# A hybrid attention and RWKV-7 layer: another order and other ring slots for the planned region

## The chip, the cores and the metric

The kernel runs on one core of one Trainium2 chip. The metric is the device time of one execution in microseconds; the time before is the median of three executions. The engines are named as in the profile: PE multiplies matrices (PEld is its loading of weights), DVE, ACT and POOL work on vectors, SP issues most of the transfers.

## The reference

A decoder layer runs attention and a recurrence beside each other on the same normalized tokens (16 meta tokens ahead of 512 of x, width 1024, 16 heads of 64):

```python
h = layer_norm(concat([meta, x]), ln0_g, ln0_b)                  # 528 x 1024
proj = h @ w_in[l]
q, k, v, zr, gate_att, gate_rwkv = split(proj)
att = swa_one(q, k, v, rel_bias, sinks)      # window 128, T5 bias, one sink a head
rw = rwkv7_time_mix(zr, ...)                 # see below
merged = sigmoid(gate_att) * att + sigmoid(gate_rwkv) * rw
h = layer_norm(ALPHA * h + merged @ w_out[l], ln1_g, ln1_b)
ff = square(relu(h @ w_ff1[l])) @ w_ff2[l]                        # 1024 -> 4096 -> 1024
h = layer_norm(ALPHA * h + ff, ln2_g, ln2_b)
return h[:, N_META:]
# the recurrence, for each head with a state S of 64 x 64:
S = S * w_t + (S @ -kk_t)[..., None] * (kk_t * a_t) + v_t[..., None] * k_t
y_t = S @ r_t
```

All of it is in float32.

## The kernel before

Each float32 product is made of three faster ones. A weight tile `wraw` is fetched by SP (L606, 512 KB), ACT casts it to a rounded high part `whi` (L611), DVE takes the difference `wlo` (L613), and `three` (L453 to L456) multiplies high by high, high by low and low by high with the likewise split tokens `hhi` and `hlo` (made by L815 and L817). The rows of one weight tile are used for two blocks of tokens, of 258, 264, 266 or 512 columns. Smaller products (scores, inverses, the recurrence) are plain fp32 matmuls.

Up to about 570 us the work is recorded first and emitted later. `lead` normalizes x while PE runs `busy` matmuls (L688) on an identity. Then come eight head pairs, each with `rwkv` and `attention`:

- projections (dense and `shifted`), evicted by ACT (L653) and DVE (L656); exponentials, keys and gains on ACT and DVE (L924 to L977); norms by PE (L987 to L989), whose result goes through DVE L992 and L994.
- scores L1031, masked on DVE into G, NT and GR (L1039, L1041, L1045).
- the inverse of each 64-block triangle: 62 steps on POOL (L1122, L1126), transfers through DRAM into `XB`, a transpose of `XB` into `U` on DVE (L1153), `inv3` on PE (L1146), a copy by ACT (L1155), `inv4` on PE (L1151), a copy by ACT (L1157), then the folds L1166 (read by DVE L1171) and L1182 (read by DVE L1186). Beside them the meta tokens' short chain, PE L1194, L1195, L1205, L1209, L1213 with ACT's copies L1200, L1216, L1218 between.
- the recurrence over chunks: a chain of seven `link` matmuls for each pair (L1243). Behind each, DVE scales one head's half of the state (L1225) and ACT the other's (L1228), and the next link reads both.
- attention: scores L1297, bias and mask on DVE (L1302, L1303), the softmax's exponentials on ACT (L1322 to L1340), transposes L1354, outputs L1366.

Then the pairs' results are merged, multiplied by w_out (L1418 to L1420), normalized, and the first part of w_ff1 follows. From there on the MLP and the last norm are written out by hand in code that no table orders (L1601, L1605, L1704, L1798).

`Plan.op` records each operation with what it reads and writes. `Plan.order` (L354) then emits the recorded operations in the order of the table `ORDER` (L91, 3087 numbers of operations), and gives each new buffer the place in its ring that stands next in the table `SLOTS` (L222): eight PSUM banks, two wraw tiles, six halves each of whi and wlo, rows for the evicted projections, and so on. All engines take their instructions in the emitted order, so ORDER sets each engine's queue, and SLOTS which earlier readers a buffer must wait for:

```python
for n in ORDER:
    o = self.ops[n]
    assert all(q in done for q in o.deps)
    for b in o.new:
        i = next(slot)
        was = owner.get((b.ring, i))
        assert was is None or left[was] == 0
        owner[b.ring, i] = b
        b.t = rings[b.ring][i]
```

Neither table has a time in it; they are read as they stand.

Of the kernel before, what the change touches and what calls it, by code (L numbers as in the profile page):

```python
# [76 lines left out]
for _name, _c in ROWS:  # L77
# [14 lines left out]
    0, 1, 26, 2, 3, 127, 5, 128, 4, 67, 30, 29, 27, 131, 68, 6, 34, 69, 7, 36, 8, 28, 42, 243,  # L92
    37, 70, 540, 41, 9, 71, 33, 10, 43, 558, 11, 861, 44, 12, 47, 35, 13, 237, 14, 45, 15, 32, 48, 16,
    46, 17, 31, 49, 18, 19, 20, 364, 60, 21, 72, 22, 50, 23, 61, 38, 24, 51, 73, 25, 62, 52, 63, 53,
    79, 64, 55, 84, 66, 89, 54, 80, 94, 86, 65, 74, 85, 81, 56, 190, 96, 87, 57, 99, 95, 90, 88, 100,
    75, 101, 134, 58, 102, 103, 132, 76, 104, 59, 105, 82, 106, 135, 107, 77, 91, 133, 122, 97, 112, 78, 276, 83,
    92, 117, 171, 98, 109, 113, 136, 108, 114, 118, 137, 110, 93, 115, 111, 124, 138, 116, 123, 119, 139, 40, 120, 142,
    125, 121, 244, 126, 143, 39, 191, 245, 246, 192, 144, 130, 172, 129, 862, 145, 140, 236, 141, 248, 146, 247, 254, 147,
    493, 148, 249, 277, 250, 149, 278, 251, 279, 287, 252, 280, 238, 253, 296, 491, 173, 239, 541, 542, 496, 1182, 255, 812,
    241, 497, 174, 494, 256, 240, 261, 495, 257, 175, 262, 242, 297, 564, 281, 258, 282, 299, 259, 265, 283, 298, 813, 185,  # L100
    266, 264, 288, 300, 284, 180, 263, 267, 597, 289, 184, 272, 285, 260, 290, 268, 176, 301, 567, 270, 1133, 271, 183, 273,
    307, 291, 492, 182, 275, 565, 302, 1200, 269, 178, 186, 274, 308, 286, 292, 188, 313, 568, 566, 309, 293, 193, 314, 303,
    337, 315, 294, 316, 559, 322, 560, 879, 561, 317, 336, 338, 179, 329, 562, 323, 326, 569, 333, 328, 194, 330, 570, 342,
    582, 327, 339, 571, 181, 177, 341, 334, 563, 575, 340, 332, 1454, 295, 572, 583, 304, 576, 324, 584, 310, 573, 325, 365,
    586, 577, 574, 331, 600, 578, 196, 195, 343, 311, 335, 345, 579, 601, 498, 585, 580, 366, 367, 197, 598, 198, 588, 346,
    521, 305, 587, 499, 581, 863, 599, 1503, 589, 206, 543, 347, 312, 500, 348, 591, 368, 592, 369, 370, 371, 199, 372, 373,
    501, 374, 375, 522, 376, 377, 318, 200, 523, 378, 596, 201, 379, 380, 526, 381, 382, 544, 383, 207, 384, 344, 545, 385,
    208, 306, 524, 386, 319, 209, 203, 387, 525, 527, 388, 212, 214, 546, 389, 502, 390, 547, 602, 391, 603, 150, 392, 393,
    528, 394, 395, 396, 608, 397, 609, 398, 399, 217, 604, 400, 202, 401, 529, 205, 402, 204, 403, 187, 404, 349, 405, 153,
    354, 406, 215, 548, 154, 407, 216, 408, 549, 218, 409, 814, 410, 610, 411, 151, 412, 550, 210, 413, 152, 357, 414, 213,  # L110
    617, 415, 353, 551, 416, 352, 417, 211, 418, 355, 419, 611, 350, 420, 530, 421, 161, 358, 422, 423, 162, 424, 425, 605,
    426, 427, 163, 428, 606, 429, 815, 155, 430, 607, 351, 593, 219, 620, 594, 612, 164, 189, 613, 320, 590, 165, 220, 432,
    595, 614, 431, 156, 356, 621, 221, 615, 618, 157, 552, 816, 222, 616, 433, 166, 508, 223, 435, 619, 639, 321, 503, 864,
    509, 643, 506, 640, 634, 504, 505, 434, 507, 649, 685, 450, 513, 635, 158, 511, 636, 510, 637, 224, 512, 817, 1455, 225,
    159, 818, 452, 638, 226, 646, 657, 359, 647, 659, 436, 885, 227, 658, 648, 453, 228, 437, 645, 454, 650, 438, 644, 455,
    651, 439, 456, 160, 865, 660, 819, 654, 661, 440, 514, 662, 167, 663, 820, 515, 655, 516, 821, 866, 653, 451, 656, 517,
    822, 652, 686, 168, 628, 169, 360, 457, 170, 441, 362, 518, 363, 867, 458, 629, 688, 886, 687, 2096, 888, 229, 887, 361,
    630, 889, 459, 519, 869, 443, 918, 442, 230, 868, 531, 520, 870, 689, 842, 533, 690, 823, 691, 692, 231, 444, 233, 693,
    232, 694, 234, 532, 695, 696, 447, 445, 697, 698, 446, 829, 919, 699, 449, 700, 824, 701, 920, 702, 534, 448, 703, 825,
    704, 827, 460, 705, 826, 631, 706, 828, 462, 707, 832, 622, 708, 833, 830, 709, 623, 461, 710, 535, 711, 921, 463, 712,  # L120
    624, 834, 464, 465, 831, 713, 625, 835, 714, 466, 715, 626, 871, 468, 716, 467, 922, 536, 717, 836, 845, 469, 938, 718,
    872, 1134, 837, 470, 719, 720, 721, 890, 722, 471, 896, 723, 632, 724, 838, 472, 725, 891, 473, 726, 846, 897, 727, 843,
    633, 892, 728, 474, 537, 729, 664, 844, 730, 475, 666, 627, 1206, 731, 477, 476, 893, 732, 733, 478, 538, 734, 479, 480,
    735, 839, 894, 736, 481, 840, 895, 737, 482, 539, 738, 880, 739, 939, 740, 665, 741, 923, 742, 883, 743, 898, 881, 744,
    745, 483, 746, 680, 747, 841, 484, 748, 882, 749, 899, 750, 485, 486, 751, 903, 924, 1209, 904, 925, 667, 929, 900, 884,
    901, 906, 930, 487, 753, 670, 684, 908, 752, 907, 931, 668, 910, 1775, 1207, 926, 1210, 905, 932, 909, 683, 675, 1208, 933,
    754, 847, 672, 912, 914, 941, 756, 934, 682, 1135, 917, 488, 911, 848, 902, 913, 915, 489, 940, 553, 676, 490, 927, 755,
    955, 554, 916, 928, 678, 942, 852, 873, 943, 671, 555, 1239, 853, 956, 771, 935, 674, 849, 556, 679, 773, 936, 557, 673,
    850, 669, 681, 957, 757, 958, 677, 1006, 1521, 979, 937, 774, 851, 959, 758, 964, 775, 854, 759, 978, 980, 776, 965, 760,
    777, 969, 971, 761, 772, 1136, 778, 972, 762, 1240, 968, 981, 780, 975, 982, 944, 1183, 977, 984, 763, 983, 945, 764, 949,  # L130
    779, 976, 946, 967, 966, 768, 970, 1007, 765, 770, 1184, 855, 766, 2466, 2814, 1137, 950, 767, 1140, 769, 1138, 1008, 1009, 947,
    1139, 781, 1241, 1141, 1185, 783, 782, 784, 856, 785, 786, 951, 858, 1010, 787, 973, 1011, 952, 1012, 789, 948, 1013, 1242, 1244,
    788, 1014, 1015, 1243, 790, 1016, 641, 792, 791, 1245, 1163, 235, 1017, 1018, 793, 1019, 1142, 1020, 794, 795, 642, 1021, 857, 1022,
    1186, 796, 1023, 1143, 953, 1024, 797, 974, 798, 1025, 1187, 1026, 799, 1144, 859, 1027, 800, 801, 1028, 1029, 802, 860, 1030, 803,
    1031, 954, 1145, 1032, 1033, 1150, 1034, 1148, 1035, 1201, 1153, 804, 1036, 1146, 1037, 1188, 1246, 1147, 1038, 1204, 1149, 1039, 1151, 987,
    1202, 1203, 1040, 805, 1211, 1041, 1224, 1154, 1155, 1152, 1217, 1776, 1042, 1156, 1212, 1043, 1044, 1213, 806, 1045, 1157, 807, 985, 1225,
    1158, 1218, 1219, 1189, 1046, 1227, 1190, 808, 1259, 1047, 989, 1166, 1048, 2417, 1049, 960, 874, 1167, 1050, 1191, 1504, 1051, 1159, 1052,
    1053, 1214, 1054, 1164, 1055, 1220, 1056, 988, 1165, 1057, 1250, 986, 875, 1527, 1221, 1058, 1247, 1842, 1262, 1160, 1059, 1060, 1222, 996,
    1161, 1061, 1263, 1168, 1062, 1215, 1063, 999, 1064, 1216, 991, 1065, 1248, 1251, 1233, 1066, 1226, 1249, 1067, 997, 1068, 1169, 1069, 1260,
    1070, 1071, 1261, 1205, 1072, 1252, 1530, 1231, 1456, 809, 1505, 1232, 1253, 1192, 961, 1254, 1162, 1229, 1073, 1074, 1255, 1170, 990, 1531,  # L140
    994, 1824, 1228, 1235, 1193, 1230, 1457, 1234, 1223, 1458, 1171, 1075, 1459, 1238, 1256, 1077, 1237, 1460, 1276, 992, 1257, 1172, 1506, 1528,
    1461, 1277, 1258, 993, 998, 1278, 1236, 1279, 1194, 1270, 1076, 1529, 810, 1285, 995, 1280, 1292, 1299, 1288, 1301, 1286, 1484, 811, 1290,
    1462, 1293, 1300, 1289, 876, 1092, 1302, 1509, 1463, 1296, 1094, 1510, 1000, 1304, 1303, 877, 1173, 1305, 1291, 1271, 1174, 1175, 962, 1078,
    1464, 1281, 1287, 1264, 1298, 1485, 963, 1328, 1079, 1465, 1327, 1297, 1095, 1176, 1080, 1282, 1486, 1096, 1081, 1093, 1295, 1097, 1272, 1082,
    1330, 1329, 1098, 1273, 1265, 1274, 1001, 1275, 1507, 1294, 1099, 1002, 1508, 1083, 1101, 1100, 1005, 1848, 1522, 1331, 1004, 1084, 1332, 1003,
# [1887 lines left out]
```

## Time and profile before

| | us |
|---|---|
| median of three runs | 897.17 (896.90 to 897.31) |
| profiled execution, time | 897.01 |
| profiled execution, span | 895.2 |
| PE busy | 874.7 |
| DVE busy | 674.4 |
| ACT busy | 518.8 |
| POOL busy | 263.2 |

The span runs from the first to the last instruction of the profile, and 1.8 us of the time lie outside it. The mean granted clock of PE was 0.994 of full speed. Busy time of PE is from modelled ends of its matmuls, which overlap, so that short waits between two of them need not show as idle; the time from the start of one to the start of the next does show them. A row of the timeline gives start, length, engine, line, what is written and read, and in brackets the idle time ahead of it with what ended it.

### The profile page before, as it was taken

How to read it: one execution, taken by the hardware profiler on the slowest of the kernel's cores; microseconds unless marked ns; L12 is line 12 of the kernel's file. 1: busy time of each engine (PE TensorE's matmuls, PEld its weight loads, DVE VectorE, ACT ScalarE, POOL GpSimd, SP SyncE). 2: the span in 40 equal slices, each digit the busy share in tenths (PEclk: the TensorE clock that was granted, in tenths of full speed). 3: DMA queues.
4: the chain of work that ended last, by engine and by line, in shares of the span. 5: the costliest groups of instructions: out<-in, count | busy, mean ns of one | idle time of the engine just before them, and what ended most of it. 6: DMA issues, size and time to landing. Idle time of an engine off the chain costs nothing.

```text
span 895.2 us, 17524 instructions
## 1 busy us (share of the span) xinstructions
PE 874.7 (98%) x6712; PEld 768.1 (86%) x6712; DVE 674.4 (75%) x1192; ACT 518.8 (58%) x1131; POOL 263.2 (29%) x672
## 2 busy tenths in 40 slices
PE   7999999999999999999989999999999999999996
PEld 6999989888898998887878877988898989888885
DVE  6882976868868678478497689598877896788757
ACT  7854568466575494483663745765556655564710
POOL 3138164183461721822816502000010000000001
PEclk9999999999999999999989999999999999999999
DMA  7443323424143242223243631395687578576322
GB/s 272 127 130 104 86 75 107 117 64 131 55 123 101 78 109 85 84 70 101 72 109 102 197 102 59 97 299 132 178 209 216 141 202 256 133 209 165 98 91 94
DMA packets 73533, 115.87 MB, mean 129 GB/s; under 512 B 40311, under 2 KB 47737, under 8 KB 69481
## 3 DMA queue, kind: packets, MB, share of 16 engines
q1 hardware_dynamic: 69728, 98.89, 35.5%
q0 software_dynamic: 2880, 14.68, 9.0%
q8 instruction: 53, 0.87, 0.4%
q10 hardware_dynamic: 840, 1.17, 0.4%
q14 instruction: 32, 0.25, 0.1%
HBM read 107.56 MB, written 8.21 MB: 129 GB/s over the span
## 4 chain that ended last, share of the span: by engine, by line
PE 90%; DVE 8%; issue 1%; ACT 1%; DMA 1%; POOL 0%; DVEq 0%; SPq 0%; ACTq 0%
PE g L454 12%; PE g L455 11%; PE g L456 11%; PE dnR L1798 7%; PE rq L1704 5%; PE tp L1704 4%; PE dnP L1798 4%; PE last L1798 4%; PE dnT L1798 3%; PE up L454 3%; PE up L455 3%; PE up L456 3%; PE g L1243 2%; PE g L1182 2%; PE g L1297 2%; PE g L1031 1%
## 5 line engine op out<-in xcount | busy, mean ns | idle before, releaser
L454 PE MATMUL g<-hhi,whi 128*128 128x512 f32 (+3 forms) x640 | 213.1, 333 | 0.2 <-DVE GR L1045 0.2
L455 PE MATMUL g<-hlo,whi 128*128 128x512 f32 (+3 forms) x640 | 204.0, 319 | 1.6 <-DVE hlo L817 1.6
L456 PE MATMUL g<-hhi,wlo 128*128 128x512 f32 (+3 forms) x640 | 203.6, 318 | 0.0
L454 PEld LDWEIGHTS g<-hhi,whi 128*128 128x128 f32 x640 | 121.0, 189 | 12.6 <-issue 2.2
L455 PEld LDWEIGHTS g<-hlo,whi 128*128 128x128 f32 x640 | 121.2, 189 | 9.6 <-DVE hlo L817 2.1
L456 PEld LDWEIGHTS g<-hhi,wlo 128*128 128x128 f32 x640 | 120.9, 189 | 8.5 <-DVE wlo L613 0.2
L613 DVE TENSOR_TENSOR wlo<-wraw,whi 128x512 fp32r<-128x512 f32 x126 | 88.3, 708 | 30.4 <-ACT whi L611 29.9
L1122 POOL TENSOR_TENSOR ftmp<-Xf,Nf 108x84 f32<-108x84 f32 (+23 forms) x248 | 86.8, 350 | 74.9 <-DMA Nf<-Nd 45.9
L611 ACT CAST whi<-wraw 128x512 fp32r<-128x512 f32 x126 | 77.0, 619 | 54.0 <-PE g L455 24.6
L1126 POOL TENSOR_TENSOR Xf<-Xf,ftmp 108x84 f32<-108x84 f32 (+23 forms) x248 | 89.6, 361 | 19.0
L1788 POOL DMA_DIRECT2D braw<-in_w_ff_dram x12 | 10.7, 890 | 206.1 <-DVE wlo L1605 87.2
L1228 ACT ACTIVATE Z<-g,PC 64x64 f32<-64x64 f32 x64 | 19.7, 308 | 65.2 <-DVE Z L1225 39.9
L1267 POOL TENSOR_TENSOR rs<-rs,mhalf 128x8 f32<-128x8 f32 (+1 forms) x9 | 14.9, 1659 | 76.2 <-DVE rs L1266 76.2
L1605 DVE TENSOR_TENSOR wlo<-wraw,whi 128x1024 fp32r<-128x1024 f32 x22 | 26.9, 1222 | 13.2 <-ACT whi L1601 10.6
L1225 DVE TENSOR_SCALAR Z<-g,PC 64x64 f32<-64x64 f32 x64 | 17.6, 274 | 23.3 <-PE g L1243 20.8
L1601 ACT CAST whi<-wraw 128x1024 fp32r<-128x1024 f32 x22 | 22.9, 1042 | 17.5 <-PE dnR L1798 8.7
L1605 DVE TENSOR_TENSOR wlo<-braw,whi 128x1024 fp32r<-128x1024 f32 x25 | 30.5, 1219 | 2.4 <-ACT whi L1601 2.4
L1605 DVE TENSOR_TENSOR blo<-braw,bhi 128x1024 fp32r<-128x1024 f32 x25 | 30.5, 1219 | 1.6 <-ACT bhi L1601 1.5
L1601 ACT CAST whi<-braw 128x1024 fp32r<-128x1024 f32 x25 | 26.3, 1053 | 5.4 <-PE rq L1704 4.6
L656 DVE SCALAR_TENSOR_TENSOR res<-g,vc,res 128x256 f32<-128x256 f32 (+2 forms) x34 | 16.2, 481 | 17.0 <-ACT res L653 16.8
L1601 ACT CAST bhi<-braw 128x1024 fp32r<-128x1024 f32 x25 | 26.3, 1051 | 3.4 <-DMA braw<-in_w_ff_dram 3.4
L454 PE MATMUL up<-h1hi,whi 128*128 128x512 f32 x72 | 28.1, 390 | 0.0
(532 smaller groups left out, 2469.6 us busy)
## 6 DMA issues: line engine op xcount, KB each, us to landing
wraw<-in_w_in_dram SPq DMA_DIRECT2D x52, 512.0 KB
braw<-in_w_ff_dram SPq DMA_DIRECT2D x19, 1024.0 KB
wraw<-in_w_ff_dram SPq DMA_DIRECT2D x32, 512.0 KB
braw<-in_w_ff_dram POOLq DMA_DIRECT2D x12, 1024.0 KB, 8.8
wraw<-in_w_out_dram SPq DMA_DIRECT2D x14, 256.0 KB
Nf<-Nd SPq DMA_DIRECT2D x24, 144.0 KB
res<-in_x_dram SPq DMA_DIRECT2D x4, 512.0 KB
G<-in_consts_dram SPq DMA_DIRECT2D x16, 128.0 KB
```

Of the source, the lines that this page charges most:

```text
L454: pe.matmul(ps, whi, xhi, start=first, stop=False)
L455: pe.matmul(ps, whi, xlo, start=False, stop=False)
L456: pe.matmul(ps, wlo, xhi, start=False, stop=last)
L611: AC(512, lambda hi=hi, qs=qs: act.copy(hi.t, raw.t[:, qs]), plain=True, r=[raw], w=[hi], new=[hi])
L613: f = lambda hi=hi, lo=lo, qs=qs, e=e: e.tensor_tensor(lo.t, raw.t[:, qs], hi.t.bitcast(F32), op=ALU.subtract)
L1122: sub(nj * nt, lambda s=s, nj=nj, nt=nt, tv=tv: pool.tensor_tensor(tv(), Xf.t[:, 0:nj, s : s + 1].to_broadcast([NB, nj, nt]), Nf.t[:, s : ...
L1126: sub(nj * nt, lambda s=s, nj=nj, tv=tv: pool.tensor_tensor(Xf.t[:, 0:nj, s + 1 :], Xf.t[:, 0:nj, s + 1 :], tv(), op=ALU.add), port=1, r=[ ...
L1228: op("ACT", 335, lambda: act.activation(Z.t[H2[1], c, 1, :], src(1), AF.Copy, scale=PC.t[H2[1], last : last + 1]), r=[ps, PC], w=[(Z, ("s" ...
L1601: act.copy(like(s["r"][0][:, :n], s["x"]), s["x"])
L1605: dve.tensor_tensor(lo, s["x"], hi.bitcast(F32), op=ALU.subtract)
L1704: pe.matmul(o, l[:, ks], r[:, k], start=start and k == c == 0, stop=stop and k == 3 and c == 2, skip_group_check=True)
L1798: pe.matmul(acc[b], l[:, as_], r[:, ws], start=first and i == 0 and q == 0, stop=last and i == NP - 1 and q == 2, skip_group_check=True)
```

## The change

Both tables are replaced by others of the same length; no other line differs, and every line number stays:

```diff
 ORDER = [
-    0, 1, 26, 2, 3, 127, 5, 128, 4, 67, 30, 29, 27, 131, 68, 6, 34, 69, 7, 36, 8, 28, 42, 243,
...
+    131, 132, 0, 27, 6, 26, 2, 134, 67, 133, 68, 135, 1, 41, 69, 7, 8, 9, 10, 11, 3, 12, 13, 14,
...
```

So the same operations run, in another sequence on each engine and with other buffers. Where that shows is best seen in the engines' rows at three places. A row gives the line, the operation, what is written and read, the shape, and how often it stands in succession.

PE in the recurrence of pair 5, before. `Z` is the state, `G` the chunk's matrix; the L1096 rows are transposes, and L454 to L456 a projection:

```order
L1031 MATMUL g<-G_143,BK_140 128x128 x8
L1243 MATMUL g<-Z_180,G_144 128x128
L1096 MATMUL g<-con,res_127 128x128 x4
L1243 MATMUL g<-Z_180,G_144 128x128 x3
L454 MATMUL g<-hhi,whi 128x512
L455 MATMUL g<-hlo,whi 128x512
L456 MATMUL g<-hhi,wlo 128x512
```

and in the new order, where L1366 are outputs of attention:

```order
L1031 MATMUL g<-G_143,BK_140 128x128 x16
L1243 MATMUL g<-Z_179,G_144 128x128
L1366 MATMUL g<-pall_194,vtok_216 64x128 x2
L1366 MATMUL g<-pown_195,vdif_218 64x128 x2
L1366 MATMUL g<-pall_194,vtok_216 64x128 x2
L1366 MATMUL g<-pown_195,vdif_218 64x128 x2
L1243 MATMUL g<-Z_179,G_144 128x128 x2
L454 MATMUL g<-hhi,whi 128x512
L455 MATMUL g<-hlo,whi 128x512
L456 MATMUL g<-hhi,wlo 128x512
```

Two links in succession are left there instead of three, and where two stood at the end of this chain there is a projection between now.

PE in pair 6's inverse, before (`U` is what L1153 transposed, `XB` the inverse's blocks):

```order
L1205 MATMUL g<-SVm_166,AKm_168 16x64 x2
L1297 MATMUL g<-khi_214,e_133 128x256 x4
L1209 MATMUL g<-RHm_174,XTm_176 16x64 x2
L1146 MATMUL g<-U_185,NT_162 32x32 x16
L1213 MATMUL g<-SVm_166,BTm_172 64x64 x2
L1151 MATMUL g<-XB_181,U_185 32x32 x16
L454 MATMUL g<-hhi,whi 128x266
L455 MATMUL g<-hlo,whi 128x266
L456 MATMUL g<-hhi,wlo 128x266
```

and in the new order:

```order
L1205 MATMUL g<-SVm_166,AKm_168 16x64 x2
L1146 MATMUL g<-U_185,NT_162 32x32 x16
L454 MATMUL g<-hhi,whi 128x266
L455 MATMUL g<-hlo,whi 128x266
L456 MATMUL g<-hhi,wlo 128x266
L454 MATMUL g<-hhi,whi 128x266
L455 MATMUL g<-hlo,whi 128x266
L456 MATMUL g<-hhi,wlo 128x266
L1209 MATMUL g<-RHm_174,XTm_177 16x64 x2
L1151 MATMUL g<-XB_181,U_185 32x32 x16
```

Between L1146 and L1151, with ACT's copy between them, there now stand six matmuls of 266 columns and the meta chain's L1209.

DVE at the same place, before:

```order
L1045 TENSOR_TENSOR GR_165<-g,con 64x4x64
L1370 SCALAR_TENSOR_TENSOR e_134<-e_134,g 128x512
L1039 TENSOR_TENSOR NT_163<-g,dv_154 64x256
L977 SCALAR_TENSOR_TENSOR res_127<-res_126,vc,e_132 128x512
L1039 TENSOR_TENSOR NT_163<-g,dv_154 64x256
L1153 STREAM_TRANSPOSE U_185<-XB_181 32x256 x2
L1198 TENSOR_TENSOR BTm_172<-g,dvm_155 48x128
L1039 TENSOR_TENSOR NT_163<-g,dv_154 64x256
```

and in the new order, where L1302 is attention's mask:

```order
L1039 TENSOR_TENSOR NT_163<-g,dv_151 64x256
L1045 TENSOR_TENSOR GR_165<-g,con 64x4x64
L1041 TENSOR_TENSOR G_144<-g,con 64x8x64
L613 TENSOR_TENSOR wlo<-wraw,whi 128x512
L1045 TENSOR_TENSOR GR_165<-g,con 64x4x64
L1153 STREAM_TRANSPOSE U_185<-XB_181 32x256 x2
L1045 TENSOR_TENSOR GR_165<-g,con 64x4x64
L1041 TENSOR_TENSOR G_144<-g,con 64x8x64
L1198 TENSOR_TENSOR BTm_172<-g,dvm_155 48x128
```

The transpose L1153 has moved from among pair 7's masks of the scores L1039 (`NT`) to behind all four of them.

ACT ahead of pair 5's inverse, before (L1340 scales the softmax's rows, L1200 and L1216 copy for the meta chain):

```order
L1101 COPY Z_180<-g 64x4x64
L963 COPY BK_140<-BK_140 64x8x64
L1101 COPY Z_180<-g 64x4x64 x2
L1200 COPY SVm_167<-g 16x128
L1089 COPY GR_165<-g 64x4x64
L653 ACTIVATE res_127<-g,drv 128x264
L1013 CAST rk_136<-e_133 128x512
L1216 COPY RHm_175<-g 16x128
L1155 COPY U_185<-g 32x256 x2
```

and in the new order:

```order
L1276 ACTIVATE z_206<-g,vc 128x512
L1089 COPY GR_164<-g 64x4x64
L611 CAST whi<-wraw 128x512
L1358 COPY pall_194<-g 128x512
L611 CAST whi<-wraw 128x512
L1340 ACTIVATE sb_193<-sb_193,sm_197 128x128 x4
L1200 COPY SVm_167<-g 16x128
L653 ACTIVATE e_131<-g,drv 128x264
L1155 COPY U_185<-g 32x256 x2
```

Ahead of L1155 there are now two casts of weights and an eviction for pair 6 (L653), and the second half of the softmax's scaling L1340 stands close to it, where short copies and one eviction stood.

At the very start, SP's first transfer is now the tile of weights of the first projection (L606, wraw), ahead of meta (L693) and the four blocks of x (L682); before, it was the eighth, behind them. Its casts on ACT and its differences on DVE are now the first work of both on data.

318 rows, old and new, of tables (ORDER, SLOTS) are left out of this document.

## The prediction

> **What bounds the kernel now.** I read the busy table first, then the chain that ended last, then the windows, and last the waits of PE. The busy table and the chain's shares by engine:
>
> ```profile
> PE 874.7 (98%) x6712; PEld 768.1 (86%) x6712; DVE 674.4 (75%) x1192; ACT 518.8 (58%) x1131; POOL 263.2 (29%) x672
> PE 90%; DVE 8%; issue 1%; ACT 1%; DMA 1%; POOL 0%; DVEq 0%; SPq 0%; ACTq 0%
> ```
>
> PE is the bound, and since the same instructions run afterwards, all that a new order can win is PE's waiting, the time its clock was low, and what a change between kinds of matmul costs. The windows (span, PE busy with its count, granted clock, DMA share, GB/s) say where PE is idle:
>
> ```profile
> 0.00:100.00 100.00, 93.73 (x711) 1.00 0.49 146
> 400.00:500.00 100.00, 94.73 (x853) 0.97 0.37 103
> 570.00:850.00 280.00, 280.00 (x1583) 1.00 0.65 183
> ```
>
> From 570 us on run the rest of the MLP and the last norm, whose code the tables don't touch (the first half of it is in the last row): 325 us that stay. In 0 to 100 PE is idle 6.3 us, in 400 to 500 it is 5.3. That is not all, for the modelled ends of matmuls hide short waits. The waits for ACT inside the pairs, seen from PE's weight loads (total, times, longest), show some of these:
>
> ```profile
> PEld g L1243 <- ACT Z L1228: 4.7, 10, 1.0
> ...
> PEld g L1151 <- ACT U L1155: 0.8, 2, 0.6
> ...
> PEld g L1213 <- ACT XB L1157: 0.5, 2, 0.4
> ...
> PEld g L1166 <- ACT XB L1157: 0.4, 1, 0.4
> ```
>
> **The change part by part.** First the links of the recurrence. PE's timeline for pair 5 has three of them with nothing in between:
>
> ```profile
> 409.19 0.47 PE L1243 MATMUL g<-Z,G 128*128 128x128 f32 x2
> 410.37 0.49 PE L1243 MATMUL g<-Z,G 128*128 128x128 f32 x2 [0.71 <-ACT Z L1228]
> 411.57 0.49 PE L1243 MATMUL g<-Z,G 128*128 128x128 f32 x2 [0.71 <-ACT Z L1228]
> ```
>
> From one start to the next 1.18 and 1.20 us pass: the link, DVE's half of the scaling (L1225), ACT's half (L1228), the next link. PE needs some 0.95 us of other work behind each link, and where the planner put less, the rest is lost: 4.7 us by the row above. In the new order I went through all 56 links: where pairs 4 and 7 had two triples of 264 columns as cover, some 0.7 us, there is now 1.17 us or more, and in pair 5 one bare pair of links is left where three stood. That pair costs 0.9 us (by the 0.71 above, and up to 1.0 by the row's longest). Gain 3.8 us, with the cover in both cases the projections' matmuls, which run anyway. Should ACT reach L1228 late, the cover is too short again, at the same price a link.
>
> Second, pair 6's inverse, where PE stands behind DVE:
>
> ```profile
> 454.98 1.02 PE L987 MATMUL g<-con,res 128*128 128x2 f32 x8 [0.38 <-DVE res L656]
> 457.65 0.60 PE L1031 MATMUL g<-G,BK 64*128 64x128 f32 x6 [0.31 <-DVE d L992]
> 462.15 0.39 PE L1209 MATMUL g<-RHm,XTm 16*16 16x64 f32 x4
> 463.72 0.24 PE L1146 MATMUL g<-U,NT 32*32 32x32 f32 x2 [1.18 <-DVE U L1153]
> 464.19 1.06 PE L1146 MATMUL g<-U,NT 32*32 32x32 f32 x30 [0.22 <-DVE U L1153]
> 466.08 1.06 PE L1151 MATMUL g<-XB,U 32*32 32x32 f32 x32 [0.42 <-ACT U L1155]
> 462.78 0.43 DVE L1039 TENSOR_TENSOR NT<-g,dv 64x256 f32<-64x256 f32 x1
> 463.24 0.90 DVE L1153 STREAM_TRANSPOSE U<-XB 32x256 f32<-32x256 f32 x2
> ```
>
> The transpose L1153 started right behind L1039, with no idle time: it stood in DVE's queue and not at a transfer. The windows (PE, PE's loads, DVE, ACT, POOL, clock, DMA share, GB/s) show that DVE was full all along, and that the clock then fell:
>
> ```profile
> 455.00:460.00 5.00, 4.69 (x57) 4.19 (x59) 4.97 (x11) 2.59 (x7) 1.41 (x6) 1.00 0.53 141
> 460.00:465.00 5.00, 3.60 (x57) 2.76 (x56) 4.81 (x13) 0.51 (x2) 0.57 (x4) 0.92 0.46 120
> 465.00:470.00 5.00, 4.43 (x55) 3.91 (x52) 4.47 (x10) 4.13 (x9) 0.00 (x0) 0.50 0.63 193
> ```
>
> The new order runs the end of pair 6's preparation earlier and stands two triples of 266 columns between L1146 and L1151 and two more behind L1151, where there was one short or none. Of DVE's work, 24.7 us belonged to 20 us of PE work here (each instruction counted with its own duration); it is spread over 30 us now. So I count the five waits above, 1.8 us of the inverse and 0.7 of L987 and L1031 before it, as gone: 2.5 us. What is late next there is DVE again, at pair 6's scores.
>
> Third, the clock. In the low stretch, and for comparison near 272 us, two neighbours of the same shape each:
>
> ```profile
> 468.53 0.43 PE L455 MATMUL g<-hlo,whi 128*128 128x266 f32 x1
> 468.76 0.42 PE L456 MATMUL g<-hhi,wlo 128*128 128x266 f32 x1
> 272.83 0.29 PE L456 MATMUL g<-hhi,wlo 128*128 128x266 f32 x1
> 272.95 0.28 PE L454 MATMUL g<-hhi,whi 128*128 128x266 f32 x1
> 400.31 0.69 PE L1151 MATMUL g<-XB,U 32*32 32x32 f32 x32
> ```
>
> The start-to-start time is 0.23 against 0.12 us. Twelve such lie in the stretch (1.3 us), and 62 small ones of the inverse took 2.12 us where at full clock they would take 1.34 (0.8); with L1213 and part of L1166 about 2.5 us, an estimate between 2.1 (these two alone) and 3.4 (half of the 6.8 us of low clock). I take the drop as gone with the waits that went ahead of it. The Trainium skill, "TensorE: Matmul & The Clock Gate" (sections "Part 1: The HAM clock gate" and "Why this matters for your kernels"), lays a drop to one whole idle window of about 3.4 us and asks for no idle gaps above about 3 us; the trace disagrees, since here no wait was over 1.18 us and PE was busy 3.60 of 5 us. By the page no stall that I foresee could lower the clock, and the term for new stalls would be a little smaller; by the row a run of narrow matmuls with a wait of one microsecond can.
>
> Fourth, the inverses of the other pairs. The rows for L1151, L1213 and L1166 sum to 1.7 us, of which 0.6 was pair 6's. The new order has 1.0 us of cover or more in each, but in pair 5 L1209 and L1213 now stand next to each other and wait for ACT's copy between them, some 0.3 us. Gain 0.8.
>
> Fifth, changes of the kind of matmul. A 512-column fp32r matmul behind an fp32 one costs
>
> ```profile
> 271.11 0.48 PE L454 MATMUL g<-hhi,whi 128*128 128x512 f32 x1
> 271.43 0.40 PE L455 MATMUL g<-hlo,whi 128*128 128x512 f32 x1
> 271.66 0.39 PE L456 MATMUL g<-hhi,wlo 128*128 128x512 f32 x1
> ```
>
> 0.32 us instead of 0.23. Counted along PE's rows, there are 38 changes between fp32r and fp32 fewer and 4 changes of tiling fewer. Were each worth 0.09, that is 3.8 us at most; but the fp32 matmul that follows another kind starts sooner by about as much, so I take 0.5 (ends 0 and 3.8).
>
> Sixth, the lead. The first wraw block, 512 KB, now goes ahead of meta and x on SP, and ACT's two casts and DVE's two differences for it stand ahead of the layer norm. Before, DVE started at once when x came, and PE later waited for hlo (timeline, the first window, and the group of DVE's differences):
>
> ```profile
> 5.93 1.29 DVE L728 BATCH_NORM_STATS2 stx<-res 128x6 f32<-128x512 f32 x2 [5.93 <-DMA res<-in_x_dram]
> 20.68 0.39 PE L455 MATMUL g<-hlo,whi 128*128 128x264 f32 x1 [1.43 <-DVE hlo L817]
> 0.00:10.00 10.00, 5.50 (x24) 5.21 (x25) 3.39 (x9) 6.99 (x16) 4.13 (x19) 1.00 0.82 275
> L613 DVE TENSOR_TENSOR wlo<-wraw,whi 128x512 fp32r<-128x512 f32 x126 | 88.3, 708 | 30.4 <-ACT whi L611 29.9
> ```
>
> 512 KB at 275 GB/s are 1.9 us by which x can come later; against it, 1.4 us of DVE and 1.2 us of ACT work leave the crowded 10 to 20 us, and the 1.43 us wait may shrink. I take 0, ends -1.4 and +1.9.
>
> Seventh, waits that the new order makes. Nothing in the trace shows them; I looked for them by adding each engine's durations along PE's rows. ACT is the worst: ahead of pair 5's inverse (L1155, L1157) it gets two softmaxes, exponentials and five casts close together. Its groups (busy, mean ns) and its window before:
>
> ```profile
> L611 ACT CAST whi<-wraw 128x512 fp32r<-128x512 f32 x126 | 77.0, 619 | 54.0 <-PE g L455 24.6 <-DMA wraw<-in_w_in_dram 15.5 <-PE g L1420 5.8
> L1326 ACT ACTIVATE sb<-sb,sm 128x128 f32<-128x128 f32 x64 | 24.9, 391 | 0.3
> L1326 ACT ACTIVATION_READ_ACCUMULATOR sb<-sb,sm 128x1 f32 x64 | 12.1, 189 | 0.0
> L1340 ACT ACTIVATE sb<-sb,sm 128x128 f32<-128x128 f32 x64 | 20.4, 394 | 3.1 <-DVE sm L1334 3.1
> 380.00:400.00 20.00, 20.00 (x187) 18.32 (x187) 15.55 (x34) 17.33 (x47) 5.11 (x22) 1.00 0.26 69
> ```
>
> Eight of L1326 with their reads (4.6 us), eight of L1340 (3.2), five of L611 (3.1) and some 14 us of copies and activations make 24.8 us for 20 us of PE work; before, ACT was busy 17.33 of these 20. It could arrive up to 4.8 us late, less what of it can start early (in the 10 us ahead it has only 1.7 us to do). From 430 to 450 it is 22.7 us for 20, ahead of pair 6's scores. Ends 0 and 4.8 + 2.7 = 7.5; I take 3.5, half, since ACT's queue is nearly empty ahead of the first and PE's order has 1.0 us of cover behind L1146.
>
> The sum: -3.8 - 2.5 - 2.5 - 0.8 - 0.5 + 0 + 3.5 = -6.6 us. The profiled execution took 897.01 us (span 895.2), the median of the runs is 897.17, so both give 890.5.
>
> **The rivals.** (a) Slower: ACT is as late as it can be at both places, 4.8 and 2.7 us, and each time PE waits in the midst of 64- and 32-row matmuls, so that the clock falls for a while as at 464 us (2.5 us each): +12.5 instead of +3.5, or 899.4. It decides as soon as ACT's lateness and its clock drops eat more than the 10.1 us won. For it speaks that ACT's work cannot be hurried and that pair 5's inverse, scores and folds are a long stretch of narrow matmuls; against it that much of that ACT work has its inputs long before. (b) No change: the gains come, but DVE becomes what PE waits for in its new crowded places. Along PE's rows I count 12.2 us of DVE work in 90 to 100, 11.4 in 280 to 290, 12.5 in 330 to 340 and 11.5 in 440 to 450, each of 10; were each excess a wait, +7.6 beside +3.5 for ACT less 1 us of overlap, and the time 897. Against it speaks that most of them follow a slack stretch (3.4 us at 80 to 90, 6.0 at 320). (c) More: no new waits, the clock whole, and the lead and the mode changes at their good ends: -9.6 - 1.4 - 2.0 = -13, or 884.
>
> **How the numbers follow.** The forecast's case, a gain with part of it given back, 887 to 894, holds 0.52; (c) and what lies below 887 hold 0.17; a small gain of 894 to 895.4 holds 0.05. Within 0.2% (1.8 us, about what a measurement of this kernel can tell from no change) lie (b) and weak forms of (a) with 0.11, and above 899 lies (a) with 0.15. So faster 0.74, same 0.11, slower 0.15. The range leaves out the worst of (a) and the best of (c): 883.5 to 898.
>
> **What would show it.** Links: PE's loads wait for ACT Z L1228 about once and under 1.2 us in total. Pair 6: no wait of L1146 for L1153 over 0.3 us and granted clock 1.00 from 400 to 500. ACT: waits of L1151, L1166, L1182 or L1031 for ACT between 395 and 455 of up to 3.5 us in all. Lead: x's first statistics start near 7.5 us, and the first projection no later than 2 us after where it was. I am wrong if the clock falls elsewhere, or if PE's idle time up to 570 us does not fall by about half.

## The result and the profile after

The new order takes 909.85 us (median of 4 runs, 908.63 to 913.52) against 897.04 for the old: a ratio of 1.0149, 95% interval 1.012 to 1.0179. It is slower by 12.8 us, where 6.6 less were forecast. The profiled execution took 909.41 us (span 906.5). Its runs also lie further apart than those of the old order, which stay within 0.5 us here (within 2.5 to 5 us in the later rounds). All medians are of runs in the faster state; one run of e13 (924.53 us, granted clock 0.977) was in a slower one and isn't counted.

The busy table after:

```profile
PE 875.9 (97%) x6712; PEld 768.8 (85%) x6712; DVE 676.6 (75%) x1192; ACT 518.2 (57%) x1131; POOL 292.7 (32%) x672
```

PE, DVE and ACT do the same as before to within 2.2 us of busy time. POOL is busy 292.7 us where it was 263.2, with the same 672 instructions. Two groups hold nearly all of that; first of the old order, then of the new:

```profile
L1126 POOL TENSOR_TENSOR Xf<-Xf,ftmp 108x84 f32<-108x84 f32 (+23 forms) x248 | 89.6, 361 | 19.0
L1122 POOL TENSOR_TENSOR ftmp<-Xf,Nf 108x84 f32<-108x84 f32 (+23 forms) x248 | 86.8, 350 | 74.9 <-DMA Nf<-Nd 45.9 <-DMA wraw<-in_w_in_dram 11.5
```

```profile
L1126 POOL TENSOR_TENSOR Xf<-Xf,ftmp 108x84 f32<-108x84 f32 (+23 forms) x248 | 108.5, 437 | 18.4
L1122 POOL TENSOR_TENSOR ftmp<-Xf,Nf 108x84 f32<-108x84 f32 (+23 forms) x248 | 97.5, 393 | 137.2 <-DMA Nf<-Nd 97.1 <-DMA G<-in_consts_dram 13.1 <-DMA bias<-tbd 9.1
```

These are the 62 steps of each pair's inverse: 176.4 us in all before, 206.0 after, on the same operands. Where PE waits (line, releaser, total, times, longest), first two rows of the old order, then the new:

```profile
PE g L1243 <- ACT Z L1228: 2.2, 3, 0.8
...
PE g L1146 <- DVE U L1153: 1.4, 2, 1.2
```

```profile
PE g L688 <- DMA con<-in_consts_dram: 5.1, 1, 5.1
PE g L1273 <- issue: 4.4, 1, 4.4
PE g L1146 <- DVE U L1153: 4.0, 4, 2.0
PE g L1194 <- ACT e L1376: 1.7, 1, 1.7
PE g L776 <- ACT sb L770: 1.4, 1, 1.4
PE g L1151 <- ACT U L1155: 1.0, 1, 1.0
PE g L1205 <- ACT SVm L1200: 1.0, 1, 1.0
...
PE g L1243 <- ACT Z L1228: 0.7, 1, 0.7
```

The links wait 0.7 us where they waited 2.2, and pair 6's L1146, whose two waits made up the 1.4 us, no longer waits. But L1146 waits in pairs 0 and 5, and DVE's transpose ahead of it no longer stands in DVE's queue. It waits for its transfer, which it never did before (here the new order's row of what DVE was idle for before L1153):

```profile
  DMA XB<-xtd: 7.1, 7
```

From the end of a pair's loop to the start of its first transpose the old order has 12.8 to 18.1 us; the new order has 6.1 to 16.4, least in pairs 0 and 5 (6.1 and 6.5), the two where PE then waits at L1146.

And in place of one stretch of low clock ahead of the MLP (464 to 471 us) there are three (107.3 to 114.1, 407.7 to 417.9 and 506.7 to 513.5 us), each with waits at or near its start. The windows (span, PE busy, granted clock, DMA share, GB/s):

```profile
105.00:115.00 10.00, 7.93 (x102) 0.66 0.39 128
400.00:420.00 20.00, 16.77 (x210) 0.74 0.33 88
500.00:515.00 15.00, 10.62 (x40) 0.77 0.43 130
```

Why POOL's steps take longer is seen by laying POOL's rows beside DVE's at one place, pair 5's loop:

```profile
383.18 0.38 POOL L1126 TENSOR_TENSOR Xf<-Xf,ftmp 108x91 f32<-108x91 f32 x1
383.63 0.74 POOL L1122 TENSOR_TENSOR ftmp<-Xf,Nf 108x84 f32<-108x84 f32 x1
384.45 0.70 POOL L1126 TENSOR_TENSOR Xf<-Xf,ftmp 108x84 f32<-108x84 f32 x1
385.23 0.66 POOL L1122 TENSOR_TENSOR ftmp<-Xf,Nf 108x77 f32<-108x77 f32 x1
385.97 1.99 POOL L1126 TENSOR_TENSOR Xf<-Xf,ftmp 108x77 f32<-108x77 f32 x1
388.03 0.33 POOL L1122 TENSOR_TENSOR ftmp<-Xf,Nf 108x80 f32<-108x80 f32 x1
```

```profile
383.50 2.20 DVE L613 TENSOR_TENSOR wlo<-wraw,whi 128x512 fp32r<-128x512 f32 x3
385.62 0.29 DVE L956 SCALAR_TENSOR_TENSOR AXm<-res,drv,Pm 64x16 f32<-64x16 f32 x1
385.84 0.67 DVE L613 TENSOR_TENSOR wlo<-wraw,whi 128x512 fp32r<-128x512 f32 x1
386.44 0.69 DVE L946 SCALAR_TENSOR_TENSOR e<-res,res 128x528 f32<-128x528 f32 x1
387.06 0.69 DVE L947 TENSOR_TENSOR res<-res,res 128x528 f32<-128x528 f32 x1
```

A step that takes 0.35 us alone takes 0.7 us beside each L613, and 1.99 us beside L613, L946 and L947 in succession. All of these have two operands in SBUF. A fit over all 992 steps of both traces (each step's duration beyond the shortest of its line and shape, against the time that each DVE line ran beside it) gives 0.7 us of stretch for each us of L613, and at most 0.1 for L656, L1186, L1302 and L1041, which read PSUM. Summed, the stretch is 26 us in the old order and 56 in the new: the new one has 40 us of L613 beside loops where the old order has 30, and more of L946, L947, L952 and their like.

The Trainium skill, "SBUF — State Buffer" (section "SBUF: two separate sides"), states that DVE with two SBUF inputs and a POOL instruction that reads SBUF exclude each other for the length of the instruction; these rows agree (0.35 us becomes 1.99).

### The profile page after: what moved, and what is told of

The parts are those of the page before. It is cut to its first block, busy times and chain, and to the rows that moved or that the text cites. A ratio compares the mean times of both kernels' runs of the same rounds, so it can differ in the third digit from the quotient of the medians.

```text
span 906.5 us, 17479 instructions
## 1 busy us (share of the span) xinstructions
PE 875.9 (97%) x6712; PEld 768.8 (85%) x6712; DVE 676.6 (75%) x1192; ACT 518.2 (57%) x1131; POOL 292.7 (32%) x672
## 5 line engine op out<-in xcount | busy, mean ns | idle before, releaser
L454 PE MATMUL g<-hhi,whi 128*128 128x512 f32 (+3 forms) x640 | 211.1, 330 | 0.0
L456 PE MATMUL g<-hhi,wlo 128*128 128x512 f32 (+3 forms) x640 | 203.4, 318 | 0.5 <-DVE wlo L613 0.5
L1122 POOL TENSOR_TENSOR ftmp<-Xf,Nf 108x84 f32<-108x84 f32 (+23 forms) x248 | 97.5, 393 | 137.2 <-DMA Nf<-Nd 97.1
L454 PEld LDWEIGHTS g<-hhi,whi 128*128 128x128 f32 x640 | 120.9, 189 | 9.3 <-issue 0.9
L456 PEld LDWEIGHTS g<-hhi,wlo 128*128 128x128 f32 x640 | 120.7, 189 | 9.3 <-DVE wlo L613 0.9
L1126 POOL TENSOR_TENSOR Xf<-Xf,ftmp 108x84 f32<-108x84 f32 (+23 forms) x248 | 108.5, 437 | 18.4
L613 DVE TENSOR_TENSOR wlo<-wraw,whi 128x512 fp32r<-128x512 f32 x126 | 89.9, 723 | 30.2 <-ACT whi L611 20.0
L611 ACT CAST whi<-wraw 128x512 fp32r<-128x512 f32 x126 | 76.2, 618 | 58.1 <-DMA wraw<-in_w_in_dram 30.6
L1228 ACT ACTIVATE Z<-g,PC 64x64 f32<-64x64 f32 x64 | 19.8, 309 | 67.9 <-PE g L1243 40.5
L1225 DVE TENSOR_SCALAR Z<-g,PC 64x64 f32<-64x64 f32 x64 | 17.5, 274 | 36.4 <-ACT Z L1228 22.6
L1267 POOL TENSOR_TENSOR rs<-rs,mhalf 128x8 f32<-128x8 f32 (+1 forms) x9 | 14.4, 1602 | 46.8 <-DVE rs L1266 46.8
L1418 PE MATMUL g<-whi,hhi 128*128 128x512 f32 x64 | 27.9, 436 | 0.5 <-DVE e L1380 0.5
L653 ACT ACTIVATE res<-g,drv 128x264 f32<-128x264 f32 (+1 forms) x32 | 14.9, 476 | 23.0 <-PE g L456 22.6
```

The lines of the kernel that those rows point to most:

```text
L454: pe.matmul(ps, whi, xhi, start=first, stop=False)
L456: pe.matmul(ps, wlo, xhi, start=False, stop=last)
L611: AC(512, lambda hi=hi, qs=qs: act.copy(hi.t, raw.t[:, qs]), plain=True, r=[raw], w=[hi], new=[hi])
L613: f = lambda hi=hi, lo=lo, qs=qs, e=e: e.tensor_tensor(lo.t, raw.t[:, qs], hi.t.bitcast(F32), op=ALU.subtract)
L1122: sub(nj * nt, lambda s=s, nj=nj, nt=nt, tv=tv: pool.tensor_tensor(tv(), Xf.t[:, 0:nj, s : s + 1].to_broadcast([NB, nj, nt]), Nf.t[:, s : ...
L1126: sub(nj * nt, lambda s=s, nj=nj, tv=tv: pool.tensor_tensor(Xf.t[:, 0:nj, s + 1 :], Xf.t[:, 0:nj, s + 1 :], tv(), op=ALU.add), port=1, r=[ ...
```

## The experiments

Each changes the old or the new order in one respect; what a kernel leaves out is said in its expectation. Times are medians, with the ratio to the old order's runs beside them and its interval.

**Is it POOL's loops?** In e1 and e2 the 60 steps behind a loop's first two are left out:

```diff
-            sub(nj * nt, lambda s=s, ...: pool.tensor_tensor(
+            sub(nj * nt, lambda s=s, ...: None if s else pool.tensor_tensor(
```

In e3 and e4 the first ten multiplications are done twice, with the same result:

```diff
-            sub(nj * nt, lambda s=s, ...: pool.tensor_tensor(tv(), ..., op=ALU.mult), ...
+            sub(nj * nt, lambda s=s, ...: [pool.tensor_tensor(tv(), ..., op=ALU.mult) for _ in range(2 if s < 10 else 1)], ...
```

> The new order with 60 of the 62 POOL steps of each pair's inverse left out (its output is therefore not the layer's). Theory POOL: the new order loses because POOL ends its inverse loops late (its steps stretch beside DVE's L613), so that DVE's transpose L1153, PE's L1146 and L1194 and POOL's own L1267 come late; without the steps the waits at 105, 232, 404 and 504 us (about 11.5 us) and the clock drops behind three of them go: 892, range 888 to 896. Rival ORDER (ACT's and DVE's queues are what PE waits for, POOL only looks late): 904 to 910. Rival LEAD (the first transfers): 908.

> The old order with the same 60 steps left out in each pair. Theory POOL: the old order has 13 to 18 us between a loop's end and the transpose, so its loops aren't on the path: 894 to 897. Rival ORDER: the same. If POOL's steps cost both orders alike (contention with DVE at large), it falls as much as the new order does, to about 885.

> The old order with ten POOL multiplications of each pair's loop done twice (the same result), some 4 us more in each loop. Theory POOL: absorbed by the slack of 13 to 18 us, of which the transfers need about 7: 897 to 899. Rival (no slack matters, POOL's load itself costs): +4 or more.

> The new order with the same 4 us more in each loop. Theory POOL: pairs 0, 2 and 5 and the step L1267 behind pair 7's loop have no slack, so each pays about 4 us, the others less: 920 to 930. Rival ORDER: 910 to 914.

Measured: e1 886.44 us (0.9879, 0.9862 to 0.9897), e2 896.62 (0.9992, 0.9982 to 1.0002), e3 917.16 (1.0218, 1.0187 to 1.0249), e4 919.91 (1.0251, 1.0232 to 1.0271). Without the loops the new order is 10.2 us faster than the old, and its waits of PE shrink. The three largest that are left:

```profile
PE g L688 <- DMA con<-in_consts_dram: 5.5, 1, 5.5
PE g L455 <- DVE hlo L817: 0.9, 3, 0.4
PE g L1243 <- ACT Z L1228: 0.7, 1, 0.7
```

The clock stays whole up to the MLP. So the loss hangs on POOL's loops: 23.4 us of the new order's time, and nothing clear of noise of the old one's. But e3 was a miss: I had taken the 13 to 18 us between the end of a loop and the transpose for slack, and some 3.4 us more in a loop cost the old order 20 us. That POOL's load itself costs this much is e3's rival; e2 speaks against it, for there nearly all of that load goes and nothing is gained. What the trace of e3 shows is lateness: L1267 and other POOL work stand behind steps, and weight transfers stand on SP behind L1130, which waits for the loop's end (SP waited for L1126 48 us there, 40 before). PE then waited 3.0 us at L1273 and 4.2 for whi and wlo. How the 20 us divide among these was not measured. The old order too is cut to the length that its loops have.

**Length, or something else?** e5, e9 and e10 replace all but a loop's first two steps by fills that read nothing:

```diff
-            sub(nj * nt, lambda s=s, ...: pool.tensor_tensor(tv(), ...), ...
+            sub(nj * nt, lambda s=s, ...: pool.tensor_tensor(tv(), ...) if s == 0 else [pool.memset(tmp.t, 0.0) for _ in range(nt_)], ...
-            sub(nj * nt, lambda s=s, ...: pool.tensor_tensor(Xf..., tv(), op=ALU.add), ...
+            sub(nj * nt, lambda s=s, ...: pool.tensor_tensor(Xf..., tv(), op=ALU.add) if s == 0 else [pool.memset(Xf.t, 0.0) for _ in range(nx_)], ...
# fills of tmp and of Xf in each step: e5 2 (1 from step 20 on) and 1; e9 1 and 2; e10 2 and 2
```

> The new order with all but the first two POOL steps of each loop replaced by fills that read nothing (the inverse's values are left out), made so that a loop lasts about 28 us by the trace's fill times, as the old order's loops do. Theory STRETCH (the loops are late because POOL's reading steps stand still beside DVE instructions with two operands in SBUF): the fills don't stretch, 888 to 894. Rival PLACE (the loops' place in the new order is too late at any usual length): 902 to 910.

> The new order with fills in place of POOL's steps again (the inverse's values are left out), now longer: about 27.6 us a loop by the fills' times, as the old order's loops are (27 to 29 without their gaps), with nothing to read in SBUF. Theory STRETCH (the new order is right for loops of the old length, and loses by the 3 to 5 us that each loop is stretched): 887 to 893. Rival (a loop of this length is already too late in the new order): 900 to 907.

> The same with 31.3 us a loop, the length that the steps have in the new order (30.6 to 32.6 us in most pairs). Theory STRETCH: the length alone brings the loss back, 904 to 912. Rival (not the loops' length but the standing still itself, or POOL holding up DVE): as the run with 27.6 us, within 3 us.

Measured: e5 886.27 us (0.9875, 0.9862 to 0.9888), but its loops came out shorter than meant, 19 to 22 us in five of the eight pairs; e9 889.35 (0.9914, 0.9893 to 0.9934) with loops of 28 to 31 in six; e10 931.4 (1.0376, 1.0344 to 1.0409) with 35 to 40 in seven, longer than meant. The fills' own length hardly depends on what DVE does (min, median, max in ns, e9):

```profile
L1129 POOL MEMSET Xf<- x480: 383/392/440, 68.4 to 492.7; 108x352 f32 x160
L1125 POOL MEMSET ftmp<- x240: 169/178/199, 68.3 to 490.9; 108x96 f32 x120
```

So with loops of about the old order's length the new order keeps most of its gain. In e10 it is length that takes it away, and not DVE being held up by POOL: DVE is busy 668.5 us there, 666.1 in e9 and 676.6 in the new order. PE waits for the pairs' transposes in e10 as in the new order (its L1148 and L1155 are L1146 and L1153 here):

```profile
PE g L1148 <- DVE U L1155: 9.3, 6, 3.0
```

Fills of just the new order's length, 33.9 us, were not run.

**Is it L613?** e11 and e16 make it read one operand, e17 makes that as long as it was:

```diff
-                lo.t, raw.t[:, qs], hi.t.bitcast(F32), op=ALU.subtract
+                lo.t, raw.t[:, qs], 2.0**-13, None, op0=ALU.mult      # tensor_scalar; e17: again on 224 columns
```

> The new order with DVE's L613 made to read one operand instead of two (the low part of the weights is left out, a scaled copy stands in for it), POOL's steps whole. If one operand in SBUF lets POOL go on, POOL's steps lose some 60% of their stretch (busy 206 to about 175 us) and the time is 888 to 898; if the instruction holds POOL up all the same, 905 to 911, unless it is shorter than 0.7 us.

> The old order with L613 reading one operand (0.44 us instead of 0.71; the low part of the weights is left out). Theory POOL HELD UP: what the new order won by this edit came from POOL's loops, so the old order, which does not wait for them, gains only what DVE's relief is worth around 455 to 470 us: 892 to 896. Rival (DVE's relief is what counts): 876 to 885, as much as in the new order.

> The new order with L613 as two one-operand instructions of 512 and 224 columns, together about as long as the two-operand one (0.7 us); the low part of the weights is left out. Theory POOL HELD UP: 887 to 894, POOL's stretch well below 54 us. Rival (DVE's relief): 903 to 910.

Measured: e11 887.53 us (0.9893, 0.9869 to 0.9917), e16 893.18 (0.9951, 0.9932 to 0.997), e17 890.94 (0.9935, 0.9912 to 0.9958). The same edit is worth 22 us in the new order and 3.7 in the old, and 19 of the 22 us remain when DVE has as much to do as before (busy 675.6 us). But these edits change a second thing: L613 no longer reads `whi` and so doesn't wait for ACT's cast L611, for which DVE stood idle 20.0 us ahead of L613 in the new order and 29.9 in the old; in e11, e16 and e17 no such wait is left. How much of the 22 us is owed to that, these three can't tell; e18 below keeps the wait. POOL's steps in e11:

```profile
L1126 POOL TENSOR_TENSOR Xf<-Xf,ftmp 108x84 f32<-108x84 f32 (+23 forms) x248 | 98.8, 398 | 18.4
L1122 POOL TENSOR_TENSOR ftmp<-Xf,Nf 108x84 f32<-108x84 f32 (+23 forms) x248 | 87.8, 354 | 126.9 <-DMA Nf<-Nd 87.4 <-DMA G<-in_consts_dram 12.3 <-DMA md<-z 9.3
```

186.6 us instead of 206.0 (188.7 in e17): the one-operand form still holds POOL up, 0.4 to 0.5 us for each us by the same fit, and it is shorter. The 60% of the stretch that I expected to go were 35% (56 to 36 us; 38 in e17).

**Can it be had back with everything computed?** e18 halves each L613:

```diff
-            f = lambda ...: e.tensor_tensor(lo.t, raw.t[:, qs], hi.t.bitcast(F32), op=ALU.subtract)
+            f = lambda ...: [e.tensor_tensor(lo.t[:, n], raw.t[:, qs][:, n], hi.t.bitcast(F32)[:, n], op=ALU.subtract)
+                             for n in (slice(0, 256), slice(256, 512))]
```

> The new order with each L613 in two halves of 256 columns, the whole computation. If POOL gets in between the halves: its stretch falls from 54 to 30 to 45 us, DVE's L613 grow by the waits for POOL, and the time is 893 to 905. If the sum counts: stretch and time as before, 908 to 915, with some 0.1 us more of DVE for each.

Measured: 897.52 us (1.0011, 0.9997 to 1.0025). That is 12.3 us less than the new order, and level with the old. POOL's steps:

```profile
L1126 POOL TENSOR_TENSOR Xf<-Xf,ftmp 108x84 f32<-108x84 f32 (+23 forms) x248 | 100.5, 405 | 18.4
L1122 POOL TENSOR_TENSOR ftmp<-Xf,Nf 108x84 f32<-108x84 f32 (+23 forms) x248 | 92.9, 375 | 129.9 <-DMA Nf<-Nd 67.8 <-DMA md<-z 32.2 <-DMA G<-in_consts_dram 12.0
```

193.4 us, between 206.0 and e11's 186.6, and the stretch is 43 us: this fits POOL getting in between the halves. L613 waits for ACT's cast as before (23.2 us), and DVE is busier, with 252 pieces of 0.42 us in place of 126 of 0.68 (medians) and 686.5 us in all; the gain of 12.3 us comes in spite of that.

e13 to e15 take other work off POOL, with everything computed: the copies L999 to L1008 go to DVE (in e14 in the old order), and in e15 the addition L1277 too:

```diff
-                    pool.tensor_copy(dv.t[...], d1.t[...])
-        op("POOL", 1260, spread, ...)
+                    dve.tensor_copy(dv.t[...], d1.t[...])
+        op("DVE", 1260, spread, ...)
# spread_x alike; e15: L1277 by DV and dve instead of PO and pool
```

> The new order with the nine small copies for each pair that spread the norms (L999 to L1008) done by DVE instead of POOL, in the same places of the order; the whole computation. POOL loses some 1.9 us a pair, and the masked scores that feed its loop come 0.6 us or more earlier. Theory POOL LENGTH: half or more of the way from 910 to 887, so 888 to 899. Rival (DVE, which takes on 0.6 us a pair, gives it back, or POOL's length isn't the cause): 905 or more.

> The old order with the same copies on DVE. Theory POOL LENGTH: nothing waits there for POOL at its present length: 896 to 898. Rival (POOL costs both orders): 890 to 894.

> As the new order with the copies on DVE, and the addition L1277 (1.3 us, six of them) on DVE too. If POOL's queue still binds: 2 to 4 us less than with the copies alone. If not, or if DVE's two-operand addition stretches POOL's steps as much as it relieves them: the same within 1.5 us.

Measured: e13 912.71 us (1.0179, 1.0153 to 1.0204), e14 905.41 (1.0084, 1.0071 to 1.0097), e15 913.94 (1.0161, 1.013 to 1.0192). All missed. Inside the loops nothing changed (a mean of 34.2 us in e13, with 56 us of stretch), and taking 2 us a pair off POOL outside them gained nothing, while DVE's 12 us more cost even the old order 7 us. Why DVE's small copies cost that much stays open.

**Single moves in the order.** e6 moves one POOL instruction in the new order, e7 one DVE instruction in the old, e8 spreads pair 5's links in the old. The numbers are operations of the table ORDER:

```diff
# e6: 12 steps of pair 7's loop (2655 to 2666) from ahead of L1267 (2412) to behind it
# e7: L1153 of pair 6 (2362) from behind L1039 (2580) to ahead of L1039 (2570)
# e8: L1366 (2143, with DVE's L1370, 2144) behind the second link, the projection parts
#     (2426, 2427, with ACT's 2428) one link earlier, half of L1297 (2429) ahead of the last link
```

> The new order with one POOL instruction moved: pair 6's L1267 goes ahead of 12 steps of pair 7's loop that stood before it. Theory POOL QUEUE: PE's wait of 4.4 us at L1273 goes, and with it the clock drop behind it (about 2 us more): 901 to 905. Rival: the wait moves on to pair 7's inverse, whose loop ends 1.7 us later: 908 to 910.

> The old order with one DVE instruction moved: pair 6's transpose L1153 goes ahead of two masks L1039 and of L977. Theory of the prediction (it stood in DVE's queue, and the wait behind it lowered the clock): 1.2 us of wait and about 2.5 us of low clock go, 893 to 894. If the clock falls all the same: 895.5 to 896. Rival (its transfer was late too): 897.

> The old order with pair 5's links set apart: attention's outputs L1366, the two projection parts and half of the scores L1297 go between them, so that one bare pair of links is left of three. Prediction's first term, by pair: 2 x 0.7 to 2 x 1.0 us less: 895.2 to 895.8. Rival (the work put between is then late for DVE and ACT, which wait instead): 897.

Measured: e6 910.54 us (1.0143, 1.0127 to 1.016), e7 897.4 (0.9997, 0.9986 to 1.0008), e8 901.4 (1.0047, 1.0029 to 1.0064). In e6 and e7 the wait that was aimed at went and others came. In e6 PE waits 3.2 us at L1419 for DVE's wlo, in e7 (where L1146 waits no more) these two, and the clock fell as before (for 6.83 us from 462.5):

```profile
PE g L1213 <- DVE BTm L1198: 1.2, 1, 1.2
PE g L454 <- DVE GR L1045: 0.9, 1, 0.9
```

In e8 the links' wait did not go: 2.4 us in two places, the longest 1.4, where it was 2.2 in three. DVE's L1370, which was moved with L1366 and waits for it, stands ahead of the next link's L1225 in DVE's queue, so that ACT's L1228 starts 2.9 us behind the one before, against 1.2. L1297 waited 1.2 us for a mask L1041, and a second clock drop came at 420 us. DVE is busy 14.3 of the 15 us from 455 to 470 us in the old order; that this load is why no single move helps in e7 is argued, not shown.

**The lead.** e12 is e1 with the first tile of weights (SP 131, ACT 132 and 134, DVE 133 and 135) moved behind x and its statistics:

```diff
# ORDER: 131, 132, 0, 27, 6, ...  ->  0, 27, 6, ..., 4, 131, ..., 62, ..., 73, 132, 133, 134, 135, ...
```

> The new order without the loops (60 of 62 steps left out, as in the run of 886.4 us) and with the first tile of weights behind the blocks of x again, its casts and differences behind the first statistics. Theory LEAD (512 KB ahead of everything cost up to 1.9 us): 884.5 to 885.5. Rival (hidden): 886.4 within 0.5.

Measured: 886.01 us (0.9874, 0.9857 to 0.9892), the same as e1's 886.44 within their intervals of about 1.6 us to each side. PE waits 3.2 us for `con`, as in the old order, where e1 has 5.5, and nothing comes of it. Both are kernels without the loops; with them the lead was not run alone.

**Loop length and time together.** Length is from the start of a loop's first step to the end of its last in the traces, as a mean over the eight pairs, with what stands between the steps on POOL:

| kernel | mean loop, us | time, us |
|---|---|---|
| new order, e5 (short fills) | 25.0 | 886.3 |
| new order, e11 (one operand) | 31.6 | 887.5 |
| new order, e9 (fills) | 31.6 | 889.4 |
| new order, e17 (one operand, same length) | 31.9 | 890.9 |
| new order, e18 (halves) | 32.5 | 897.5 |
| new order | 33.9 | 909.9 |
| new order, e4 (ten steps twice) | 36.6 | 919.9 |
| new order, e10 (longer fills) | 38.3 | 931.4 |
| old order | 29.7 | 897.0 |
| old order, e3 (ten steps twice) | 33.1 | 917.2 |

In the new order time stays nearly flat up to about 32 us and then climbs by 12 us for 1.4 us of loop, and more slowly above. The new order's own loops are 2 us beyond the bend. Of the new order's other kernels e6 (33.9 us, 910.5) and e13 (34.2, 912.7) fit this, and e15 (33.5, 913.9) lies above it. In the old order e7 (29.9, 897.4), e8 (29.7, 901.4), e14 (29.9, 905.4) and e16 (28.9, 893.2) differ in time at nearly one length. So the length of the loops decides much of the time, not all.

## Why the prediction was wrong, point by point

The step that failed is the seventh, "waits that the new order makes". It looked for them "by adding each engine's durations along PE's rows", found ACT worst, took 3.5 us for it, and put POOL at nothing. With the low clock behind them these waits are 23.4 us (909.85 less e1's 886.44), and they hang on POOL's loops. There were two faults. POOL was left out, since at 29% busy it looked idle; but a loop is one link of a chain (masked scores, transfer, 62 steps, transfers, transpose, inverse), and a chain is as late as its slowest link, however idle its engine. And the sums took each instruction's duration as fixed, when POOL's depend on what DVE runs beside it. That could be seen before: in the old order L1122 and L1126 have stretched steps too, up to 0.87 and 1.03 us where the median is 0.33.

- First term, links: 3.8 us forecast. PE's loads waited 4.7 us for ACT's Z and 0.4 for DVE's half; after, 1.3 and 1.6. So 3.4 us went as forecast and 1.2 came back through DVE, 2.2 net. e8, which set pair 5's links apart in the old order, gained nothing.
- Second and third, pair 6 and the clock there: right in place. L1146 of pair 6 doesn't wait, and the clock is whole from 450 to 500 us. But "I take the drop as gone with the waits" held for that drop only: three others came behind POOL's late loops. That the wait at L1146 lowered the clock isn't shown either: in e7 it is gone, others stand in its place, and the clock falls all the same.
- Together with the fourth and fifth terms 10.1 us of gain were forecast; without the loops the new order is 10.2 us faster (e1 against e2). The sum fits that; no term is shown by itself, and with the first at 2.2 net an agreement to 0.1 us is in part luck. In the fifth it isn't the fp32 matmul that starts sooner: in the old order's trace an fp32r matmul of 512 columns starts 0.03 us behind the L1243 ahead of it (median of 22), where the second matmul of a link starts 0.11 us behind the first.
- Sixth, the lead: 0 forecast. x's first statistics start at 7.45 us (5.93 before), the first projection 0.9 us later, and e12 shows no difference clear of noise in the time.
- Rival (a), ACT's lateness: 899.4 was its price, and it did not happen by that mechanism. ACT's waits at L1151, L1194 and L1205 go when the loops go, so they followed the late inverse. Rival (b), DVE in crowded stretches: DVE mattered, through POOL.
- Both signs of being wrong came: the clock fell elsewhere, and PE's idle time did not fall by half but rose from 13.0 us (570 us less 557.0 busy) to 23.1 (582 less 558.9).
- Against the Trainium skill, "TensorE: Matmul & The Clock Gate" (section "Why this matters for your kernels"), which asks for no idle gaps above about 3 us, the forecast held with the rows: three more drops came where the longest single wait was 1.0, 2.0 and 4.4 us, and only the last is above 3.

Not settled: how the 23 us divide between waits and low clock place by place. An estimate of the clock's share against the old order: 23.9 us at half clock (6.83, 10.24 and 6.83) against 6.83 cost at most half of the difference, 8.5 us.

## What to carry to other kernels

Before an order is judged by sums of busy time, find the serial chains that run over the least busy engine, and give each its length and its slack; an order that is tight for everything else makes that chain the bound, and some 2 us more of loop cost about 20 here (e9 and e17 against the new order). Where one engine stretches another's instructions, a duration belongs to a neighbourhood and not to the instruction: compare the mean of a group with its median and its shortest, and look at what ran beside the long ones. A long instruction that holds another engine up can be cut in pieces, which gave back 12.3 us here with everything computed and left the new order level with the old.

## What the runs showed of the hardware

- Beside DVE instructions with two operands in SBUF, POOL's reading steps of 0.35 us took up to 2.1 us in the new order; POOL's fills in e9, which read nothing, kept medians of 178 and 392 ns and at most 199 and 440.
- With each L613 in two halves of 256 columns (e18) POOL's steps stretched less in sum than with one of 512 (43 against 56 us over the kernel).
- Low clock, half of full speed, came in lengths of 3.41 (e3, e18), 6.83 (both orders), 10.24 (new order, e4) and 13.65 us (e6) ahead of the MLP, all multiples of 3.41 to within 0.01, as in every other run here that had any.
